# Three pairs of gate tiles as seven-product blocks, and two products of each block pair added up in PSUM

## The chip, the cores and the metric

One Trainium2 chip, one of its NeuronCores. The metric is the time of one execution on the device in microseconds (us), the median of some runs. A NeuronCore has TensorE (PE, the matrix array), VectorE (DVE), ScalarE (ACT), GpSimd (POOL) and SyncE (SP); each works through its own queue in order, and they wait for each other by semaphores. Matmuls read SBUF and add up in PSUM, which has 8 banks; DVE and ACT read PSUM, DMA queues move data between DRAM and SBUF.

## The reference

One encoder layer for 576 columns (512 frames of a prompt and 64 of a sample), model width 1024, FFN width 2816, all in fp32:

```python
x = x + 0.5 * swiglu_ffn(rms_norm(x, ffn1_norm), ffn1_w_gate_up, ffn1_w_down)
h = rms_norm(x, mix_norm)
p = h @ w_in
a_b, a_c, a_v, b_u, gate_a, gate_b = jnp.split(p, cuts, axis=-1)
a_conv, new_a = causal_depthwise_conv(a_c * a_v, hist_a, conv_a_w)
y_a = (a_b * a_conv) @ w_a_out
glu = b_u[..., :D_B] * jax.nn.sigmoid(b_u[..., D_B:])
b_conv, new_b = causal_depthwise_conv(glu, hist_b, conv_b_w)
b_act = jax.nn.silu(layer_norm(b_conv + conv_b_bias, conv_b_ln_g, conv_b_ln_b))
y_b = b_act @ w_b_out
merged = jax.nn.sigmoid(gate_a) * y_a + jax.nn.sigmoid(gate_b) * y_b
x = x + merged @ w_out
x = x + 0.5 * swiglu_ffn(rms_norm(x, ffn2_norm), ffn2_w_gate_up, ffn2_w_down)
```

and a last RMSNorm; the convolutions' last inputs are outputs too.

## The kernel before

Features lie on the 128 partitions, 8 tiles of 128 for the model width, the 576 columns along the free axis in two halves of 288. Weights are the stationary operand. For fp32 accuracy each operand is split into a high and a low part, and a product takes three matmuls: high x high, high x low, low x high. A **plain tile** (`product`: 128 output features, all 576 columns) is 8 x 3 x 2 = 48 matmuls of 288 columns, in one PSUM tile `mm` of two banks; the pool `mmps` has four of them. A finished product is put in the list `behind` and evacuated by `take` when the next one has been issued.

A **block pair** computes two output tiles by Winograd's form of Strassen's scheme: the weights of two tiles in 2 x 2 blocks (output tile by half of the 8 input tiles), the operand in 2 x 2 blocks (half of the input tiles by half of the columns), seven products (`block`, 12 matmuls into a single bank that `bank` hands out from two-bank tiles) in place of eight: 84 matmuls for 96. It needs sums of weight blocks (made on DVE for each pair as the weights come) and four sums of operand blocks, the forms, which the class `Forms` makes once for a stage: `combine` forms them on DVE and casts their high parts on ACT, `split` makes the low parts on DVE. Of the seven products q[0] to q[6] the two output tiles are put together from half tiles: the tile q1 is q[0] copied out by ACT, u2 comes of q[1] and q1, u4 of q[2] and u2, u3 of q[3] and u2; then a half of the first output comes of q[4] and q1 and its other half of q[5] and u4, a half of the second of q[2] and u3 and its other half of q[6] and u3, all on DVE. Semaphores guard PSUM by whole two-bank tiles.

The program runs in this order: FFN 1 (groups of gate/up tiles, of which 18 are block pairs, each followed by the down projection); branch b's value and gate tiles ("p", 4 and 3) and branch a's ("p", 1, 2, 0); then branch a's gate tiles ("p", 5, j) alternating with its output tiles ("ya", j); branch b's gate tiles ("p", 6, j); branch b's output "yb", two plain pairs and two block pairs; the output projection "o"; FFN 2 (21 block pairs). While PE works on the p and ya tiles, DVE runs branch b's 31-tap convolution and the LayerNorm behind it. These are small steps in the list `work`, which `fill` hands out between products by a planner's clock. The LayerNorm goes through `advance` in stages: gathering the sum, mean `mu`, then for each of 8 tiles `center` (subtract the mean on DVE, square on ACT, add to the running sum on DVE), the variance's sum on PE, and its reciprocal root; then `swish`.

The order on each engine is the order in which the code is written, kept by `Ordered`. Weights come through `Stream`: SP loads raw chunks to six buffers, ACT casts the high part, and the low part is made either by ACT (times -1) and an accumulating DMA that POOL issues, or by DVE; it works six units ahead of PE. All instructions go through one helper, so all have the line L88 in the profile; they are told apart by their tiles: `mm` PSUM, `tmp` work tiles, `u`, `g` and `act` homes of weights (`act` also of operands), `raw` loaded weights, `w` work tiles and sums of weights, `x` the residual and the merged outputs, `acc` running sums, `r` row factors.

Of the kernel before, what the change touches and what calls it, by code (L numbers as in the profile page):

```python
# [9 lines left out]
F32 = mybir.dt.float32  # L10
# [101 lines left out]
def tile_encoder_step(  # L112
# [280 lines left out]
    def plan_mixer(name, w, col, home_of=None, low="dma"):  # L393
        plan_tile(name, w, 0, (KU, KU), col, "act", home_of, low)
# [12 lines left out]
    for j in range(KT):  # L407
        plan_mixer(("p", 6, j), w_in, 6 * D + j * P, few)


# [38 lines left out]
            got += [(w, kk) for kk in range(ws.units[n][1])]  # L449
        return got  # L450

    def block(w, xs):

        q = bank()[:, :H]
        for k in range(KU):
            (whi, wlo), (xh, xl) = w, xs[k]
            for m, (l, r) in enumerate(((whi, xh), (whi, xl), (wlo, xh))):
                pe.matmul(q, l[:, k, :], r, start=k == m == 0, stop=k == KU - 1 and m == 2)
        return q


    work = []
# [180 lines left out]
    class Forms:  # L643
# [176 lines left out]
    def ffn(f, xg, sums, finish, forms, R=None, todo=()):  # L820
# [40 lines left out]
                    step(p)  # L861

        def pair(i, hs, last):
            qu, uu, t, cu = (ttile() for _ in range(4))
            q1, u2, u3, u4 = half(qu, 0), half(qu, 1), half(uu, 0), half(uu, 1)
            q = []

            def q7():
                dve.tensor_tensor(u3, q[3], u2, op=ALU.add)
                dve.tensor_tensor(half(cu, 1), u3, q[2], op=ALU.subtract)  # L870

            def gate():
                dve.tensor_tensor(half(t, 1), q[5], u4, op=ALU.add)
                dve.tensor_tensor(t, t, R, op=ALU.mult)
                sca.activation(t, t, AF.Silu)

            steps = (
                lambda: sca.copy(q1, q[0]),
                lambda: dve.tensor_tensor(u2, q[1], q1, op=ALU.subtract),
                lambda: dve.tensor_tensor(u4, q[2], u2, op=ALU.subtract),  # L880
                q7,
                lambda: dve.tensor_tensor(half(t, 0), q[4], q1, op=ALU.add),
                gate,
            )
            for n, xs in enumerate(bs):
                q.append(block(ws.get(plan[f, "s", i][n]), xs))
                if n > 0:
                    steps[n - 1]()
                if rest:
                    rest.pop(0)()  # L890

            hs.append(None)
            at = len(hs) - 1

            def up():
                if last:
                    dve.tensor_tensor(t, t, R, op=ALU.mult)
                dve.tensor_tensor(half(cu, 0), q[6], u3, op=ALU.add)
# [219 lines left out]
    def swish(i, RL, sig={}):  # L1118
# [13 lines left out]
        if 0 <= j < KT:  # L1132
            BA[j] = (BA[j], low(sig[j], BA[j]))
            forms.b.setdefault(j // 2, []).append(sig[j])

    def ga_of(j):
        def then(ps):
            t = gates[j] = ttile()
            sca.activation(halves(t), ps, AF.Sigmoid)
        return then  # L1140

    def ya_of(j):
        def then(ps):
            dve.tensor_tensor(halves(M[j]), ps, halves(gates.pop(j)), op=ALU.mult)
        return then

    stage, held = [0], [0]
# [1 line left out]
    def advance():  # L1149

        nonlocal var, mu, RL
        if stage[0] == 0 and len(C) == KT and not work:
            lnsum.gather()
        elif stage[0] == 1:
            mu = ttile()
            sca.mul(halves(mu), lnsum.total(), 1.0 / D)
            var = Sum()
            work.extend((lambda i=i: center(i, mu)) for i in range(KT))
        elif stage[0] == 2 and not work:
            var.gather()  # L1160
        elif stage[0] == 3 and not held[0]:
            held[0] = 1
            return
        elif stage[0] == 3:
            RL = rstd(var)
        else:
            return
        stage[0] += 1

    var = mu = RL = None  # L1170
    for j in range(KT):
        if j == 5:
            while len(C) < KT:
                work.pop(0)()
        product(("p", 5, j), xg, ga_of(j))
        advance()
        product(("ya", j), AB, ya_of(j))
        advance()
    take()
    sca.dma_start(hist.rearrange("(j p) n -> p j n", p=P), hst)  # L1180
    while stage[0] < 4:
        while work:
# [8 lines left out]
            work.append(lambda p=(i - 4) // 2: forms.split(p))  # L1191
    ws.ahead = 4

    def gb_of(j):
        def then(ps):
            while work and j >= 2 and len(BA) < j - 1:
                work.pop(0)()
            sg = wtile(n=T) if j < 2 else gtile(n=T)
            sca.activation(halves(sg), ps, AF.Sigmoid)
            SGB.append(sg)  # L1200
        return then

    for j in range(KT):
        product(("p", 6, j), xg, gb_of(j))
    while work:
        work.pop(0)()
# [32 lines left out]

    def block_pair(i):  # L1240
        j = 2 * i
        c1, c2, qu, uu = (ttile() for _ in range(4))
        q1, u2, u3, u4 = half(qu, 0), half(qu, 1), half(uu, 0), half(uu, 1)
        q = []

        def second():
            dve.tensor_tensor(u3, q[3], u2, op=ALU.add)
            dve.tensor_tensor(half(c2, 1), u3, q[2], op=ALU.subtract)

            if i == KU - 1:  # L1250
                MS[4], MS[5] = split(M[4]), split(M[5])

        def first():
            dve.tensor_tensor(half(c1, 1), q[5], u4, op=ALU.add)
            dve.tensor_tensor(c1, c1, SGB[j], op=ALU.mult)
            merged(j, c1)

        steps = (
            lambda: sca.copy(q1, q[0]),
            lambda: dve.tensor_tensor(u2, q[1], q1, op=ALU.subtract),  # L1260
            lambda: dve.tensor_tensor(u4, q[2], u2, op=ALU.subtract),
            second,
            lambda: dve.tensor_tensor(half(c1, 0), q[4], q1, op=ALU.add),
            first,
        )
        for n, xs in enumerate(bs):
            q.append(block(ws.get(plan["yb", "s", i][n]), xs))
            if n > 0:
                steps[n - 1]()
        dve.tensor_tensor(half(c2, 0), q[6], u3, op=ALU.add)  # L1270
        dve.tensor_tensor(c2, c2, SGB[j + 1], op=ALU.mult)
        merged(j + 1, c2)
        spare.clear()
# [164 lines left out]
```

## Time and profile before

| | |
|---|---|
| runs, median (lowest to highest) | 1294.61 us (1294.13 to 1297.48) |
| the profiled execution, its span | 1290.1 us |
| time beside the span, against the median | 4.5 us |
| mean granted TensorE clock | 0.997 |
| POOL busy | 361.6 us (28%) |
| DMA, mean | 167 GB/s |

The page gives each engine's busy time and share, then its busy tenths in 40 slices of the span; the views behind it group instructions by engine, operation and tile (count, busy time, mean ns of one, and the idle time before them with what ended it), list who waited for whom, follow the chain of work that ended last, show instructions in order of time (start, duration, what it is, and in brackets the idle time ahead of it and its releaser), and sum up busy times by stretches of time. Starts of matmuls are exact to follow PE's pace by; their ends overlap the next one's start.

### The profile page before, as it was taken

The numbers are of one execution on the slowest core, as the hardware profiler recorded it, in microseconds if no ns is written. First come the engines' busy times: TensorE is split into PE (matmuls) and PEld (weight loads), VectorE is DVE, ScalarE is ACT, GpSimd is POOL, SyncE is SP. The second block draws the span as 40 slices with busy tenths as digits, with TensorE's granted clock in tenths as the row PEclk, the third lists the DMA queues.
The fourth block names the chain that finished last, engine by engine and source line by source line (L and its number), as shares of the span: only waits on it lengthen the run. The fifth ranks groups of instructions, "written<-read, shape, count | busy, mean of one in ns | idle before, by whom it ended". The sixth has DMA issues, their size and how long they took to land.

```text
span 1290.1 us, 25702 instructions
## 1 busy us (share of the span) xinstructions
PE 1279.4 (99%) x9728; PEld 1277.5 (99%) x9728; DVE 925.1 (72%) x1539; ACT 765.5 (59%) x1359; POOL 361.6 (28%) x460
## 2 busy tenths in 40 slices
PE   9999999999999999999999999999999999999997
PEld 9999999999999999999999999999999999999997
DVE  6868668748846998888895166656867848847956
ACT  7655646646776645555444576477665655654664
POOL 0032332232333444333321221122142141241230
PEclk9999999999999999999999999999999999999998
DMA  7286787886799898788885767696687696796783
GB/s 220 70 181 154 163 180 155 177 181 149 154 224 232 174 200 173 165 172 174 172 172 124 163 142 154 151 236 145 139 175 171 151 197 151 164 204 138 158 172 97
DMA packets 286812, 215.26 MB, mean 167 GB/s; under 512 B 15456, under 2 KB 248928, under 8 KB 286688
## 3 DMA queue, kind: packets, MB, share of 16 engines
q0 software_dynamic: 56160, 92.43, 43.3%
q1 hardware_dynamic: 228784, 120.35, 32.8%
q8 instruction: 77, 1.26, 0.4%
q10 hardware_dynamic: 1744, 0.83, 0.2%
q14 instruction: 47, 0.39, 0.1%
HBM read 116.17 MB, written 4.98 MB: 94 GB/s over the span
## 4 chain that ended last, share of the span: by engine, by line
PE 92%; issue 4%; DVE 2%; DMA 1%; ACT 1%; POOL 0%; DVEq 0%; POOLq 0%; ACTq 0%
PE mm L88 92%; DVE tmp L88 0%; DMA g<-raw 0%; DMA raw<-in_w_b_out_dram 0%; DVE x L88 0%; DVE g L88 0%; DMA u<-raw 0%; ACT act L88 0%; DVE w L88 0%; POOL u L88 0%; DVE act L88 0%; ACT u L88 0%; ACT w L88 0%; ACT g L88 0%; POOL g L88 0%
## 5 line engine op out<-in xcount | busy, mean ns | idle before, releaser
L88 PE MATMUL mm<-act,u 128*128 128x288 f32 x4758 | 668.3, 293 | 0.1
L88 PEld LDWEIGHTS mm<-act,u 128*128 128x128 f32 x4758 | 638.9, 188 | 0.4 <-DMA u<-raw 0.3
L88 PE MATMUL mm<-act,g 128*128 128x288 f32 x3030 | 432.9, 294 | 0.9 <-DMA g<-raw 0.9
L88 PEld LDWEIGHTS mm<-act,g 128*128 128x128 f32 x3030 | 410.3, 188 | 1.1 <-DMA g<-raw 1.1
L88 POOL DMA_DIRECT2D u<-raw x197 | 172.3, 874 | 481.7 <-ACT u L88 317.4
L88 PE MATMUL mm<-act,act 128*128 128x288 f32 (+2 forms) x1896 | 259.9, 293 | 0.0
L88 PEld LDWEIGHTS mm<-act,act 128*128 128x128 f32 x1896 | 252.2, 188 | 0.5 <-ACT act L88 0.3
L88 ACT CAST u<-raw 128x512 fp32r<-128x512 f32 (+2 forms) x207 | 118.8, 574 | 172.0 <-PE mm L88 136.7
L88 POOL DMA_DIRECT2D g<-raw x126 | 109.9, 872 | 297.4 <-ACT g L88 242.7
L88 DVE SCALAR_TENSOR_TENSOR w<-g,prm,w 128x606 f32<-128x606 f32 x232 | 179.3, 844 | 1.4 <-ACT w L88 1.4
L88 DVE TENSOR_TENSOR tmp<-mm,tmp 128x288 f32<-128x288 f32 (+1 forms) x251 | 112.9, 459 | 70.3 <-PE mm L88 53.7
L88 ACT ACTIVATE u<-u 128x512 fp32r<-128x512 f32 (+2 forms) x197 | 116.8, 593 | 6.2
L88 ACT CAST g<-raw 128x512 fp32r<-128x512 f32 (+2 forms) x136 | 75.1, 553 | 43.9 <-DMA raw<-in_ffn_w_down_dram 17.6
L88 DVE SCALAR_TENSOR_TENSOR tmp<-mm,r 128x576 f32<-128x576 f32 x48 | 36.3, 757 | 76.6 <-PE mm L88 76.6
L88 POOL DMA_DIRECT2D act<-raw x67 | 59.1, 883 | 108.3 <-ACT act L88 94.5
L88 ACT CAST act<-tmp 128x576 fp32r<-128x576 f32 x92 | 61.9, 675 | 43.1 <-DVE tmp L88 42.1
L88 ACT CAST g<-w 128x512 fp32r<-128x512 f32 x79 | 49.0, 620 | 64.4 <-DVE w L88 58.6
L88 ACT CAST u<-w 128x512 fp32r<-128x512 f32 x81 | 50.2, 619 | 61.0 <-DVE w L88 43.6
L88 DVE TENSOR_TENSOR act<-tmp,act 128x576 fp32r<-128x576 f32 x92 | 67.5, 754 | 18.1 <-ACT act L88 16.5
L88 ACT ACTIVATE g<-g 128x512 fp32r<-128x512 f32 (+2 forms) x126 | 72.1, 572 | 4.0
L88 DVE TENSOR_TENSOR w<-raw,raw 128x512 f32<-128x512 f32 x82 | 56.2, 685 | 16.2 <-DMA raw<-in_ffn_w_gate_up_dram 11.2
L88 ACT ACTIVATE tmp<-tmp 128x576 f32<-128x576 f32 x47 | 32.2, 686 | 45.1 <-DVE tmp L88 45.0
(86 smaller groups left out, 830.6 us busy)
## 6 DMA issues: line engine op xcount, KB each, us to landing
raw<-in_ffn_w_gate_up_dram SPq DMA_DIRECT2D x171, 256.0 KB, 3.5
u<-raw POOLq DMA_DIRECT2D x140, 256.0 KB, 4.2
raw<-in_w_in_dram SPq DMA_DIRECT2D x112, 256.0 KB, 3.8
raw<-in_ffn_w_down_dram SPq DMA_DIRECT2D x96, 192.0 KB, 3.8
g<-raw POOLq DMA_DIRECT2D x69, 256.0 KB, 4.2
act<-raw POOLq DMA_DIRECT2D x61, 256.0 KB, 4.4
g<-raw POOLq DMA_DIRECT2D x43, 192.0 KB, 4.5
u<-raw POOLq DMA_DIRECT2D x41, 192.0 KB, 4.5
```

Of the source, the lines that this page charges most:

```text
L88: return self.tc.keep_in_program_order(fn(*args, **kwargs))
```

## The change

There are two parts. First, a new function `seven` runs the products of every block pair, and `block` can now be given a bank to add onto: product 4 is added to product 0's bank and product 5 to product 2's (the table `ONTO`). So that they can be, q[0] and q[2] are copied out first, by ACT. u4 is gone, and so is the addition for the first half of the first output: q[4]'s bank holds it, and ACT copies it out. A pair takes five banks in place of seven. DVE has two instructions less per pair, ACT two more. This holds for all pairs of FFN 1, yb and FFN 2.

Second, branch a's gate tiles ("p", 5, 2) to ("p", 5, 7) become three block pairs of the same kind. PE's order was p5 and ya in turn, then p6. It is now p5 tile 0, all eight ya, p5 tile 1, p6 tile 0, the three pairs, p6 tiles 1 to 7. The ya tiles from 1 on are copied out by ACT, and gated later on DVE (`gated`). The pairs' forms need the operand in one piece again: `whole` copies the high part with ACT and adds the low part by an accumulating DMA that POOL issues. The LayerNorm's stages behind the first now run between the products of the pairs (`between`).

```diff
@@ order of the weights @@
+    plan_mixer(("p", 5, 0), w_in, 5 * D)
     for j in range(KT):
-        plan_mixer(("p", 5, j), w_in, 5 * D + j * P)
         plan_mixer(("ya", j), w_a_out, j * P)
+    plan_mixer(("p", 5, 1), w_in, 5 * D + P)
+    plan_mixer(("p", 6, 0), w_in, 6 * D)
+    for i in range(1, KU):
+        plan_block(("p5", "s", i), [
+            ws.raw(w_in, h * KU * P, KU, 5 * D + j * P) for j in (2 * i + 1, 2 * i)
+            for h in range(2)
+        ], [home("act") for _ in range(7)])
@@ block and seven @@
-    def block(w, xs):
+    def block(w, xs, onto=None):
 
-        q = bank()[:, :H]
+        q = bank()[:, :H] if onto is None else onto
...
+    ONTO = {4: 0, 5: 2}
+
+    def seven(ws7, xs7, c1, c2, gate, between=None):
+        qu, uu = ttile(), ttile()
+        q1, u2, q3, u3 = half(qu, 0), half(qu, 1), half(uu, 0), half(uu, 1)
+        q = []
+
+        def second():
+            dve.tensor_tensor(u3, q[3], u2, op=ALU.add)
+            dve.tensor_tensor(half(c2, 1), u3, q3, op=ALU.subtract)
+
+        def first():
+            dve.tensor_tensor(half(c1, 1), q[5], u2, op=ALU.subtract)
+            gate()
+
+        steps = (
+            lambda: sca.copy(q1, q[0]),
+            lambda: dve.tensor_tensor(u2, q[1], q1, op=ALU.subtract),
+            lambda: sca.copy(q3, q[2]),
+            second,
+            lambda: sca.copy(half(c1, 0), q[4]),
+            first,
+        )
+        for n, xs in enumerate(xs7):
+            q.append(block(ws.get(ws7[n]), xs, q[ONTO[n]] if n in ONTO else None))
+            if n > 0:
+                steps[n - 1]()
+            if between:
+                between()
+        return lambda: dve.tensor_tensor(half(c2, 0), q[6], u3, op=ALU.add)
@@ Forms @@
+        def whole(self, p, xs):
+            self.b[p] = [wtile(n=T) for _ in range(2)]
+            for b, (hi, lo) in zip(self.b[p], (xs[p], xs[p + KU])):
+                sca.copy(b, hi.bitcast(F32))
+                pool.dma_start(b, lo.bitcast(F32), accum_op=ALU.add)
@@ the stage of p5, ya and p6 @@
-            mu = ttile()
+            mu = rpool.tile([P, T], F32, tag="r", name=nm("mu"), bufs=2)
...
+    xforms = Forms()
+    product(("p", 5, 0), xg, ga_of(0))
     for j in range(KT):
-        if j == 5:
+        if j == KT - 1:
             while len(C) < KT:
                 work.pop(0)()
-        product(("p", 5, j), xg, ga_of(j))
-        advance()
+            xforms.whole(0, xg)
         product(("ya", j), AB, ya_of(j))
-        advance()
-    take()
+        if stage[0] == 0:
+            advance()
+    for n, (b, then) in enumerate(((5, ga_of(1)), (6, gb_of(0)))):
+        for p in (2 * n, 2 * n + 1):
+            xforms.combine(p)
+            if p < KU - 1:
+                xforms.whole(p + 1, xg)
+            xforms.split(p)
+        product(("p", b, 1 - n), xg, then)
+    bs = xforms.operands(xg)
+    later = []
+
+    def gate_pair(i):
+        j = 2 * i
+        c1, c2 = ttile(), ttile()
+
+        def first():
+            sca.activation(c1, c1, AF.Sigmoid)
+            gated(j, c1)
+
+        def second():
+            final()
+            sca.activation(c2, c2, AF.Sigmoid)
+
+        def between():
+            take()
+            if later:
+                later.pop(0)()
+            advance()
+            fill()
+
+        final = seven(plan["p5", "s", i], bs, c1, c2, first, between)
+        later.extend((second, lambda: gated(j + 1, c2)))
```

What this does to the queues, at three places. On ACT of the changed kernel, behind tile ya5's evacuation: `x` rows are evacuations of ya tiles, the `COPY w<-act` rows are `whole`, and the `CAST act<-tmp` rows cast the forms that DVE makes from those `w`.

```order
L88 COPY x_96<-mm_8738 128x576
L88 CAST act_8874<-tmp_8868 128x576
L88 CAST act_8876<-tmp_8869 128x576
L88 COPY w_8878<-act_5268 128x576
L88 COPY w_8879<-act_5435 128x576
L88 CAST act_8894<-tmp_8888 128x576
L88 CAST act_8896<-tmp_8889 128x576
L88 COPY w_8898<-act_5271 128x576
L88 COPY w_8899<-act_5589 128x576
```

Nothing of this was there before; each round's copies stand behind the casts of the round ahead.

Further on in the same queue, from behind the last forms to the first gate pair's copy of q[0] (the last row): the `act` and `u` rows are weights, `tmp<-mm` and `w<-mm` the sigmoids of p5 tile 1 and p6 tile 0, `mu` the mean, `acc<-g` the first square.

```order
L88 CAST act_9007<-raw_8711 128x512
L88 ACTIVATE act_9008<-act_9007 128x512
L88 CAST u_9036<-w_9005 128x512
L88 ACTIVATE tmp_9062<-mm_8908 128x576
L88 CAST act_9072<-raw_8637 128x512
L88 ACTIVATE act_9073<-act_9072 128x512
L88 ACTIVATE w_9096<-mm_9003 128x576
L88 ACTIVATE mu_9098<-mm_9099 128x576
L88 ACTIVATE acc_9105<-g_5279 128x576
L88 CAST u_9110<-raw_8912 128x512
L88 ACTIVATE u_9110<-u_9110 128x512
L88 COPY tmp_9067<-mm_9083 128x288
```

Before, there were no pairs here, and the mean and the squares stood behind ya tiles; now eleven rows stand ahead of the copy. Between it and the copy of q[2] stand two more squares and two weight casts.

On DVE at the first yb pair, before (u2, then u4, then behind the sum `w<-raw,raw` of two weight blocks u3 and the half of the second output):

```order
L88 TENSOR_TENSOR tmp_10148<-mm_10162,tmp_10148 128x288
L88 TENSOR_TENSOR act_10194<-raw_10005,act_10193 128x512
L88 TENSOR_TENSOR tmp_10149<-mm_10196,tmp_10148 128x288
L88 TENSOR_TENSOR u_10213<-raw_10011,u_10213 128x512
L88 TENSOR_TENSOR w_10231<-raw_10158,raw_10160 128x512
L88 TENSOR_TENSOR tmp_10149<-mm_10196,tmp_10148 128x288
L88 TENSOR_TENSOR tmp_10147<-tmp_10149,mm_10196 128x288
```

and now (u2, the sum, u3, and the half of the second output from SBUF):

```order
L88 TENSOR_TENSOR tmp_10266<-mm_10280,tmp_10266 128x288
L88 TENSOR_TENSOR act_10312<-raw_10123,act_10311 128x512
L88 TENSOR_TENSOR u_10331<-raw_10129,u_10331 128x512
L88 TENSOR_TENSOR w_10349<-raw_10276,raw_10278 128x512
L88 TENSOR_TENSOR tmp_10267<-mm_10314,tmp_10266 128x288
L88 TENSOR_TENSOR tmp_10265<-tmp_10267 128x288
```

u4 is gone; u3 stands behind the same sum of weights as before.

More of the change, by code (lines that the diff above doesn't have):

```diff
@@ L1192, in tile_encoder_step @@
     ws.ahead = 4
[L1194 to L1203, printed above, removed]
+    for j in range(1, KT):
         product(("p", 6, j), xg, gb_of(j))
@@ L1241, in block_pair, with between @@
         j = 2 * i
[L1242 to L1251, printed above, removed]
+        c1, c2 = ttile(), ttile()
         def first():
[L1254 removed]
             dve.tensor_tensor(c1, c1, SGB[j], op=ALU.mult)
             merged(j, c1)
[L1258 to L1270, printed above, removed]
+        def between():
+            if i == KU - 1 and between.n == 4:
+                MS[4], MS[5] = split(M[4]), split(M[5])
+            between.n += 1
+        between.n = 0
+        seven(plan["yb", "s", i], bs, c1, c2, first, between)()
         dve.tensor_tensor(c2, c2, SGB[j + 1], op=ALU.mult)
```

57 lines of the change are left out of this document (33 added, 24 removed).

## The prediction, made before the changed kernel was run

> **What bounds the kernel now.** I read the page's head first, then PE's waits, then the chain of work that ended last.
>
> ```profile
> span 1290.1 us, 25702 instructions
> PE 1279.4 (99%) x9728; PEld 1277.5 (99%) x9728; DVE 925.1 (72%) x1539; ACT 765.5 (59%) x1359; POOL 361.6 (28%) x460
> PEclk9999999999999999999999999999999999999998
> PE mm L88 <- POOL eps L88: 1.0, 1, 1.0
> PE mm L88 <- DMA g<-raw: 0.9, 1, 0.9
> PE mm L88 <- ACT tmp L88: 0.5, 1, 0.5
> 4.81 803.97 PE mm L88 x6138
> ```
>
> PE is busy for 99% of the span, at full clock, and in all waits 2.4 us for anybody; the chain is PE without a break for its first 800 us. So time can be gained in two ways only, by fewer matmuls or faster ones, and **any new wait of PE is lost time, undiluted**. VectorE (DVE) and ScalarE (ACT) have slack on the mean, but the mean is not what counts where PE begins to wait for single instructions of theirs. The profiled execution's span is 1290.1 us; the median of the runs is 1294.61, so 4.5 us lie around the span, and I add them at the end.
>
> **Fewer matmuls.** A plain tile is 48 matmuls, a block pair 84 in place of 96. Their pace, in PE's timeline (start, duration, matmuls):
>
> ```profile
> 644.98 3.28 PE L88 MATMUL mm<-act,act 128*128 128x288 f32 x24
> 648.10 3.28 PE L88 MATMUL mm<-act,u 128*128 128x288 f32 x24
> 651.22 3.28 PE L88 MATMUL mm<-act,act 128*128 128x288 f32 x24
> ...
> 689.20 3.32 PE L88 MATMUL mm<-act,act 128*128 128x288 f32 x24
> 692.36 3.32 PE L88 MATMUL mm<-act,u 128*128 128x288 f32 x24
> 808.61 1.74 PE L88 MATMUL mm<-act,u 128*128 128x288 f32 x12
> ...
> 814.95 1.74 PE L88 MATMUL mm<-act,u 128*128 128x288 f32 x12
> 816.53 1.75 PE L88 MATMUL mm<-act,g 128*128 128x288 f32 x12
> ...
> 819.70 1.52 PE L88 MATMUL mm<-act,u 128*128 128x288 f32 x10
> ```
>
> Starts count, not the overlapping ends: a plain tile takes 651.22 - 644.98 = 6.24 us (130.0 ns a matmul), and 6.32 between the two four-matmul LayerNorm sums; a block pair takes 819.70 - 808.61 = 11.09 (132.0 ns). Two tiles become one pair: 11.09 - 12.48 = -1.39, three times. The four slow tiles between the sums were 0.08 slower each; that goes too. **-4.4 us**, and at 131.5 ns for each of the 36 matmuls it would be -4.7. That is sure, as far as PE is not made to wait.
>
> **What accumulating in PSUM moves.** DVE loses two instructions per pair, ACT gains two, in all 41 old pairs. Neither bounds. But before, block 4 wrote into a fresh bank, and now it is added onto the bank of product 0. It can't start until q1 has been copied out (ACT) and, where products 0 and 1 share a two-bank tile, until u2 has been computed (DVE); block 5 likewise waits for q3 and u3. Block 4 comes 6.34 us after the pair's start, block 5 7.92. So I ask where q1, u2 and u3 stood in each pair of before.
>
> First pair of FFN 1 (starts at 56.84), first yb pair (808.61) and first pair of FFN 2 (908.1; blocks 4 and 5 at 914.49 and 916.07):
>
> ```profile
> 63.17 1.74 PE L88 MATMUL mm<-act,g 128*128 128x288 f32 x12
> 63.41 0.39 ACT L88 COPY tmp<-mm 128x288 f32<-128x288 f32 x1
> 64.95 0.45 DVE L88 TENSOR_TENSOR tmp<-mm,tmp 128x288 f32<-128x288 f32 x1
> 818.56 0.69 DVE L88 TENSOR_TENSOR w<-raw,raw 128x512 f32<-128x512 f32 x1 [2.36 <-DMA raw<-in_w_b_out_dram]
> 819.17 0.45 DVE L88 TENSOR_TENSOR tmp<-mm,tmp 128x288 f32<-128x288 f32 x1
> 915.60 0.46 DVE L88 TENSOR_TENSOR tmp<-mm,tmp 128x288 f32<-128x288 f32 x1 [0.70 <-ACT tmp L88]
> 919.02 0.45 DVE L88 TENSOR_TENSOR tmp<-mm,tmp 128x288 f32<-128x288 f32 x1
> ```
>
> FFN 1: u2 ended at 65.40, block 4 began at 63.17: **+2.2**. yb: u3 (819.62) stands behind a sum of two weight chunks that came by DMA, block 5 began at 816.53: **+3.1**; the loads are not earlier in the changed order there. FFN 2: u2 ended at 916.06, 1.6 after block 4; u3, less the 0.37 of the subtraction that goes ahead of it, at 919.1, against a block 5 that is by then at 917.65: 1.4 more. **+3.0**. Each may be nothing, if its operand comes sooner than before, or half as long again.
>
> The other pairs, at the pair that starts at 1006.73 (blocks 4 and 5 at 1013.04 and 1014.62):
>
> ```profile
> 1011.58 0.46 DVE L88 TENSOR_TENSOR tmp<-mm,tmp 128x288 f32<-128x288 f32 x1 [0.56 <-ACT tmp L88]
> 1014.03 0.45 DVE L88 TENSOR_TENSOR tmp<-mm,tmp 128x288 f32<-128x288 f32 x1
> 1015.00 0.45 DVE L88 TENSOR_TENSOR tmp<-mm,tmp 128x288 f32<-128x288 f32 x1
> ```
>
> u2, u4, u3: u2 is 1.0 us ahead of block 4, but u3 ended at 1015.45, 0.83 late. u4 goes, which brings u3 0.37 forward; and the gate of the pair ahead, behind which u2 queues, no longer waits for a product in the other bank of its tile, some 1.3 us. I take **0** with 0.6 to spare; without that relief it is 0.46 in each of some 16 such pairs, +7 to +8.
>
> **The three gate pairs.** Here everything new meets: the operands' sums ("forms") are built late, the LayerNorm's steps are run between the products, and the evacuation of a pair sits behind both in ACT's and DVE's queues. Costs:
>
> ```profile
> u<-raw POOLq DMA_DIRECT2D x140, 256.0 KB, 4.2
> L88 ACT COPY tmp<-mm 128x576 f32<-128x576 f32 x8 | 5.0, 623 | 0.0
> L88 ACT CAST act<-tmp 128x576 fp32r<-128x576 f32 x92 | 61.9, 675 | 43.1 <-DVE tmp L88 42.1
> L88 DVE TENSOR_TENSOR tmp<-w,tmp 128x288 f32<-128x288 f32 x16 | 7.3, 454 | 0.3
> L88 ACT CAST act<-raw 128x512 fp32r<-128x512 f32 x65 | 39.7, 611 | 6.4 <-PE mm L88 3.0 <-DMA raw<-in_ffn_w_gate_up_dram 2.1 <-DMA raw<-in_w_in_dram 1.2
> L88 ACT ACTIVATE act<-act 128x512 fp32r<-128x512 f32 x61 | 38.6, 634 | 1.9
> 695.57 0.69 ACT L88 ACTIVATE tmp<-g 128x576 f32<-128x576 f32 x1 [1.49 <-DVE g L88]
> 696.29 0.76 DVE L88 TENSOR_TENSOR acc<-acc,tmp 128x576 f32<-128x576 f32 x1 [0.75 <-ACT tmp L88]
> 696.97 0.75 DVE L88 TENSOR_TENSOR g<-g,tmp 128x576 f32<-128x576 f32 x1
> ```
>
> *Forms.* Four rounds, each in series, since the next round's copies stand on ACT behind the casts of this one: two copies 1.25, the accumulating DMA's landing 4.2 (a transfer of weights of nearly this size; SBUF to SBUF as here), two DVE ops 0.91 until a cast can begin, two casts 1.35: 7.7 us. The first copy can't run before tile ya5 (ends at 644.98 + 7 x 6.24 = 688.7) is evacuated, a weight cast and a copy later, near 690.6. The last form is there at 690.6 + 4 x 7.7 = 721.4. PE reaches the pairs at 644.98 + 11 x 6.24 = 713.6, and block 1, the first to need the last form, at 715.2. That is a wait of about 6 us; with a landing of 3.3 it is 3.
>
> *Evacuation.* On ACT eleven instructions stand between the last form and the copy of q1: seven weight steps (0.61 and 0.63), two sigmoids, the mean and the first square (0.6 to 0.7 each), 6.9 us; the square waits about 1.5 more for its centering on DVE, which has weights ahead of it. Copy and u2 add 0.83: block 4 may go at about 730.6, where it stood ready at 726.9. u3 has five DVE ops (0.7 each) and a square behind it: 735.0. Pair 1 ends at 738.2, against 725 without a wait: 13.0. In the later pairs ACT has 18 ops (10.6 us) and DVE 20 (11.4 us) between one q1 and the next, as much as PE's 11.09, but they can't be packed: centering, square and running sum hand over from DVE to ACT and back (the rows above: 2.18 us a step, each engine idle for 0.75 or 1.49 of it). I followed both queues in their new order with these durations: pair 2 ends at 752.5 (3.2 late, u3 at its last block), pair 3 at 767.4 (3.8, u2, the variance's sum and u3), and the next gate tile waits 0.5 more for its bank. **+20.5 us**. From below: were the forms in time and each q1 the next thing on ACT, nothing; from above, all handed over in series, half as much again, 30.
>
> The outputs of branch a are now copied out by ACT and gated on DVE later, so 0.62 on ACT for each; between 680 and 700 it was busy for 9 us of 20:
>
> ```profile
> 680.00:700.00 20.00, 20.00 (x155) 20.00 (x155) 8.17 (x13) 9.03 (x16) 3.44 (x4) 1.00 0.59 126
> ```
>
> That hides them, **0**; their place in the queue is in the times above. The weights, loaded in the new order, I cost at nothing too: PE waited 0.9 us for them in all of before, and they run six units ahead; without that cover it would be a landing of 4.2.
>
> After the pairs, LayerNorm's output comes some 8 us later against the remaining gate tiles of branch b, whose evacuations it feeds: **+2**, 0 to 3.
>
> **The clock after a stall.** PE stands still twice in before: 1.16 us near 845, and at the very end (columns of the stretches: length, the five engines, clock, DMA):
>
> ```profile
> 845.00:845.50 0.50, 0.00 (x0) 0.00 (x0) 0.50 (x2) 0.47 (x2) 0.50 (x1) 1.00 1.05 194
> 1281.21 0.73 PE L88 MATMUL mm<-tmp,ones_r 128*128 128x272 f32 x2 [0.54 <-ACT tmp L88]
> 1283.00:1283.50 0.50, 0.00 (x0) 0.00 (x0) 0.47 (x2) 0.00 (x0) 0.00 (x0) 0.72 0.57 190
> 1283.50:1284.00 0.50, 0.00 (x0) 0.00 (x0) 0.47 (x2) 0.00 (x0) 0.00 (x0) 0.50 0.00 0
> ```
>
> Near 845 the clock stayed at 1.00; at the end it fell to half about 1.3 us after the last matmul (1281.94). The stalls above are longer than that. What the restart costs no row shows: nothing, or up to a whole block at half clock (another 1.58). Inside the gate pairs a slow block mostly runs into a later wait. For the three stalls outside I take as long at half clock as it took to fall, 0.65 each: **+2**.
>
> [...]
>
> **Sum**: -4.4 + 20.5 + 2 + 2.2 + 3.1 + 3.0 + 2 = +28.4. Span 1290.1 + 28.4 = 1318.5, time 1318.5 + 4.5 = **1323.0 us**.
>
> **The rivals.**
> *Faster: no operand is late.* It is decided at one place, block 4 of a gate pair: if q1's copy gets through ACT within 6.3 us of the pair's start, all pairs run at 11.09, and what remains is the 36 matmuls: 1290.2 us, 0.34% faster. For it: ACT is busy 59% and DVE 72%, and while PE waits once, the others catch up. Against: the order of ACT's queue, with eleven instructions ahead. **0.15**, spread over 1287 to 1297.
> *Partial.* The forms land in time (landing 3.3, weight casts ahead of them done early) and only the hand-overs remain, about 8 in the gate stage: -4.4 + 8 + 8 = 1306; 1297 to 1313. **0.20**.
> *Every second FFN pair waits* 0.46 for u3, because the relief by the bank fails: 7.5 more, 1330.5. u3's row above speaks for it, u4's removal against. **0.07**.
> *The clock gate.* Six restarts that nothing absorbs (three gate pairs, FFN 1, yb, FFN 2) run one block each at half clock, 6 x 1.58 = 9.5 in place of 2: 1330.5, and more if it takes longer. The row of the fall speaks for it, the one near 845 against it for short stalls. **0.11**.
> *The forecast*, 1313 to 1333: **0.47**.
>
> **How the numbers follow.** 0.3% is about what a measurement of this kernel can tell from no change, 1290.7 to 1298.5. Faster holds two thirds of the first rival: 0.10. Same holds the rest of it and the lower edge of the partial case: 0.07. Slower 0.83. The range goes from 1298 to 1340: it leaves out the first rival (0.15) and the upper tail of the clock's (0.03), and holds the bounds of the forms (17.5 to 23.5 in place of 20.5) and of FFN's steady pairs.
>
> **What would show it.** PE's waits in the new profile name the cause: ACT act or DVE act (forms) near 715, then ACT tmp and DVE tmp (q1, u2, u3) in 713 to 768, sum about 20; single waits for DVE tmp of 2 to 3 us at the first pairs of FFN 1, yb and FFN 2; and a granted clock below 1 behind them. PE's matmuls should be 36 fewer. The forecast is wrong if PE goes through the gate pairs without a gap (then 1290), or if PE's gaps lie in the FFN stages in every second pair.

## The result, and the profile after

The changed kernel takes 1332.12 us (median of 5 runs, 1328.62 to 1334.35) against 1294.13 us of before in the same session (5 runs, 1291.45 to 1297.48): a ratio of 1.029, 95% interval 1.027 to 1.031. Forecast were 1323.0, in a range of 1298 to 1340. It is slower by 38 us, where 28.4 were worked out.

The head of the page of the changed kernel, and PE's five longest waits in total (who was waited for, us in total, times, longest):

```profile
span 1327.7 us, 25642 instructions
PE 1286.0 (97%) x9692; PEld 1280.2 (96%) x9692; DVE 930.9 (70%) x1520; ACT 813.9 (61%) x1479; POOL 365.1 (27%) x465
PE mm L88 <- DVE tmp L88: 14.8, 10, 2.5
PE mm L88 <- ACT act L88: 8.8, 3, 6.7
PE mm L88 <- ACT tmp L88: 3.5, 3, 2.3
PE mm L88 <- DMA u<-raw: 3.5, 1, 3.5
PE mm L88 <- ACT u L88: 1.3, 1, 1.3
```

PE has 36 matmuls less, and 33.5 us of waits in all in place of 2.4. Nothing else of the head tells of it: DVE and ACT are as far from full as before. PE is "busy" for 6.6 us more with fewer matmuls; most of that is the clock, below.

Where the 37.6 us of the two profiled executions lie, by the starts of the same tiles in PE's timeline:

| from, to | before | after | difference | forecast |
|---|---|---|---|---|
| start to p5 tile 0 (FFN 1 in it) | 644.98 | 647.39 | +2.4 | +2.9 (2.2 + 0.65 of clock) |
| p5 tile 0 to p6 tile 1 (the gate pairs) | 107.47 | 130.19 | +22.7 | +16.1 (20.5 - 4.4) |
| p6 tile 1 to the first yb tile | 43.68 | 51.11 | +7.4 | +2 |
| yb to the output projection | 47.19 | 51.67 | +4.5 | +3.8 (3.1 + 0.65) |
| output projection to FFN 2's first pair | 64.83 | 63.08 | -1.7 | 0 |
| FFN 2's first pair to the end | 381.95 | 384.26 | +2.3 | +3.7 (3.0 + 0.65) |

The -1.7, which was not forecast, has two parts: before's wait near 845 (DMA g) is gone, 1.0 us, and most of the tiles go at 130.0 ns a matmul in place of 131.7 (see the end).

PE's timeline of the changed kernel through the first gate pair, blocks 0 to 6 and the LayerNorm's sum (start, duration, matmuls, in brackets the idle time ahead and its releaser):

```profile
716.03 1.74 PE L88 MATMUL mm<-act,act 128*128 128x288 f32 x12
717.61 0.69 PE L88 MATMUL mm<-tmp,ones_r 128*128 128x288 f32 x4
718.14 0.95 PE L88 MATMUL mm<-act,u 128*128 128x288 f32 x6
720.81 0.40 PE L88 MATMUL mm<-act,u 128*128 128x288 f32 x1 [1.72 <-ACT act L88]
721.60 0.53 PE L88 MATMUL mm<-act,u 128*128 128x288 f32 x2 [0.40 <-DVE act L88]
728.82 0.61 PE L88 MATMUL mm<-act,u 128*128 128x288 f32 x1 [6.70 <-ACT act L88]
...
732.80 3.25 PE L88 MATMUL mm<-act,act 128*128 128x288 f32 x12 [2.33 <-ACT tmp L88]
735.84 2.41 PE L88 MATMUL mm<-act,u 128*128 128x288 f32 x12
739.86 1.81 PE L88 MATMUL mm<-act,act 128*128 128x288 f32 x12 [1.60 <-DVE tmp L88]
744.11 3.25 PE L88 MATMUL mm<-act,u 128*128 128x288 f32 x12 [2.44 <-DVE tmp L88]
747.16 1.93 PE L88 MATMUL mm<-act,act 128*128 128x288 f32 x12
748.92 1.74 PE L88 MATMUL mm<-act,u 128*128 128x288 f32 x12
```

The waits come in the forecast's order: block 1 for the third and the fourth form (ACT act), block 4 for u2, block 5 for u3. One more, which the forecast did not name, lies between: block 2 waits for the bank that a sigmoid on ACT empties (ACT tmp). And blocks of the same 12 matmuls take 1.58 us from start to start, or up to 3.05 (744.11 to 747.16). The stretches of that time (length, PE, PEld, DVE, ACT, POOL, granted clock, DMA share, GB/s) say why:

```profile
733.00:737.00 4.00, 4.00 (x17) 4.00 (x18) 3.71 (x6) 3.14 (x6) 0.86 (x1) 0.50 0.47 100
750.00:757.00 7.00, 7.00 (x56) 7.00 (x55) 6.09 (x11) 4.57 (x9) 1.72 (x2) 1.00 0.62 121
```

Between 733 and 737 PE worked without a pause, but at half clock, 17 matmuls in 4 us where 30 go at full clock.

### The profile page after: what moved, and what is told of

The parts are those of the page before. It is cut to its first block, busy times and chain, and to the rows that moved or that the text cites. A ratio compares the mean times of both kernels' runs of the same rounds, so it can differ in the third digit from the quotient of the medians.

```text
span 1327.7 us, 25642 instructions
## 1 busy us (share of the span) xinstructions
PE 1286.0 (97%) x9692; PEld 1280.2 (96%) x9692; DVE 930.9 (70%) x1520; ACT 813.9 (61%) x1479; POOL 365.1 (27%) x465
## 4 chain that ended last, share of the span: by engine, by line
PE 85%; DVE 6%; issue 3%; ACT 3%; DMA 2%; POOL 0%; DVEq 0%; POOLq 0%; ACTq 0%
PE mm L88 85%; DVE tmp L88 2%; DMA w<-act 1%; DVE act L88 1%; ACT tmp L88 1%; DVE g L88 1%; ACT act L88 1%; DVE w L88 1%; DVE u L88 1%; ACT u L88 0%; ACT w L88 0%; DMA raw<-in_w_b_out_dram 0%; DVE x L88 0%; DVE acc L88 0%; DMA gains<-in_params_dram 0%
## 5 line engine op out<-in xcount | busy, mean ns | idle before, releaser
L88 POOL DMA_DIRECT2D g<-raw x123 | 107.2, 872 | 255.2 <-ACT g L88 153.1
L88 DVE TENSOR_TENSOR tmp<-mm,tmp 128x288 f32<-128x288 f32 (+1 forms) x181 | 83.9, 463 | 91.6 <-PE mm L88 63.0
L88 ACT CAST act<-tmp 128x576 fp32r<-128x576 f32 x100 | 67.4, 675 | 68.6 <-DVE tmp L88 67.0
L88 DVE TENSOR_TENSOR act<-tmp,act 128x576 fp32r<-128x576 f32 x100 | 73.5, 754 | 16.0 <-ACT act L88 14.4
L88 ACT CAST u<-w 128x512 fp32r<-128x512 f32 x86 | 53.2, 619 | 49.4 <-DVE w L88 34.8
L88 ACT COPY tmp<-mm 128x288 f32<-128x288 f32 (+1 forms) x140 | 56.5, 404 | 41.4 <-PE mm L88 37.4
L88 DVE TENSOR_TENSOR w<-raw,raw 128x512 f32<-128x512 f32 x88 | 60.3, 685 | 25.8 <-DMA raw<-in_ffn_w_gate_up_dram 13.0
```

The costliest lines, as they stand in the source:

```text
L88: return self.tc.keep_in_program_order(fn(*args, **kwargs))
```

## The experiments

Twelve kernels were run, in five sessions; each ratio is against runs of the kernel before on the same chip, with its 95% interval.

### The two parts apart

`acc_old` is the kernel before with `seven` and `ONTO` in its 41 block pairs and nothing else. `seven_banks` is the changed kernel with

```diff
-    ONTO = {4: 0, 5: 2}
+    ONTO = {}
...
-            lambda: sca.copy(q3, q[2]),
+            lambda: dve.tensor_tensor(u4, q[2], u2, op=ALU.subtract),
             second,
-            lambda: sca.copy(half(c1, 0), q[4]),
+            lambda: dve.tensor_tensor(half(c1, 0), q[4], q1, op=ALU.add),
```

> The kernel before with the first part of the change alone: products 4 and 5 added up in PSUM in the 41 old block pairs, no gate pairs. Theory A (a bank that is added onto is given back late, and PE waits where DVE or ACT is behind): the three places of the changed kernel come back alone, waits of PE for DVE tmp of 1.9 us in FFN 1, 2.6 in yb and 1.7 and 1.4 in FFN 2, and some 2 us at a lower clock behind them, less about 1 because the gap near 845 falls away: 1301 to 1304 us, 0.6% over before. Rival B (adding up costs nothing, all of the loss comes from the gate pairs and the new order): within 0.2% of before, and no waits of PE for DVE tmp.

> The changed kernel with the second part of the change alone: gate pairs, forms and order as changed, but all 44 pairs with seven banks each and the old steps on DVE. A: the waits at the first pairs of FFN 1, yb and FFN 2 go (9 us with the clock), and in the gate pairs the waits for DVE tmp go (about 9 us), while those for the forms (ACT act and DVE act, 10 us) and for the weights behind the pairs (5 us) stay: 1312 to 1318. B: the waits come from the queues, not from the banks; they stay where they were: 1328 to 1334.

| | median us | ratio to before |
|---|---|---|
| acc_old | 1302.98 | 1.0083 (1.0058 to 1.0109) |
| seven_banks | 1319.09 | 1.0213 (1.0185 to 1.0242) |

The two ratios are worth 10.7 and 27.5 us; together 38.2, and the whole change 37.5. By the spans of the profiled executions it is 8.5 and 25.5, together 34.0, and the whole change 37.6. So the parts add up within some 5 us, which is what the intervals leave open; that neither feeds the other at all is not shown. PE's waits, first of acc_old, then of seven_banks:

```profile
PE mm L88 <- DVE tmp L88: 7.8, 5, 2.5
```

```profile
PE mm L88 <- ACT act L88: 7.8, 2, 6.7
PE mm L88 <- ACT tmp L88: 6.6, 3, 3.7
PE mm L88 <- DMA u<-raw: 4.3, 2, 2.8
PE mm L88 <- DMA act<-raw: 2.7, 1, 2.7
```

In acc_old the waits for DVE tmp are at the first pairs of FFN 1, yb and FFN 2 and one in yb's second pair (0.4); none in the other pairs. Rival B falls: adding up in PSUM costs, though only where DVE or ACT is behind. With seven banks DVE tmp is all but gone from the gate stage too (0.3 in all), but the waits for ACT tmp rose from 3.5 to 6.6 us, a bank that an ACT evacuation holds and the LayerNorm's sum, and weights of the second pair are late. So A was right on the three places outside, while of its 9 us in the gate pairs nothing came back: from p5 tile 0 to p6 tile 1 it takes 129.9 us in place of 130.2, other operands being late instead. The time is 1 us over A's range.

### The forms

`forms_early` starts the rounds two tiles earlier, with two rounds' copies in flight; `both` does that with seven banks. `whole_dve` leaves the rounds where they were and makes them without a DMA:

```diff
-                sca.copy(b, hi.bitcast(F32))
-                pool.dma_start(b, lo.bitcast(F32), accum_op=ALU.add)
+                dve.tensor_tensor(b, hi.bitcast(F32), lo.bitcast(F32), op=ALU.add)
```

> The changed kernel with the forms' rounds begun two tiles earlier, one round ahead of each of the tiles ya6, ya7, p5 1 and p6 0, with two rounds' copies in flight. A: PE's waits for ACT act and DVE act (10 us) go; the evacuation of the pairs still queues behind the LayerNorm's steps, so waits for DVE tmp stay, and the three places outside stay: 1316 to 1324. Rival C (the forms alone are what is late in the gate stage, the rest follows from them): all 27 us of that stage go, 1303 to 1307.

> Early forms and seven banks together. A: only the weights behind the pairs are left (7 us with the clock), and part of the LayerNorm's hand-overs: 1293 to 1302. If the gate pairs' matmuls were slower in themselves (rival D: accumulation or not, a block costs more here than 131 ns a matmul), it would be over 1305.

> The changed kernel with the operand put together by one DVE addition (0.75 us) in place of ACT's copy and POOL's accumulating DMA; nothing else moved. Theory A (the landing is what made a round 9.1 us in place of 7.7): a round falls to about 4 us, PE's waits for ACT act (8.8 us) go, and the evacuation queue behind them moves up by as much, as in forms_early: 1313 to 1322. Rival F (a round's length is set by ACT's casts and their place in the queue): rounds stay over 7 us and the time over 1327.

| | median us | ratio to before |
|---|---|---|
| forms_early | 1316.36 | 1.0183 (1.0150 to 1.0216) |
| both | 1303.62 | 1.0095 (1.0064 to 1.0127) |
| whole_dve | 1313.22 | 1.0152 (1.0125 to 1.0179) |

In forms_early no wait for ACT act is left, and the time is within A's range, against C: with the forms in time, the evacuation is late all the same, 13.2 us of waits for DVE tmp in the whole kernel. The gate pairs' stage falls from 130.2 to 115.1 us. `both` came out 1.6 us over its range: PE waited 4.1 us for ACT tmp and 6.9 for weights (DMA u and DMA act), all in the gate stage and behind it, and 33 matmuls went at half clock there, 3.6 us more. Its gate pairs' stage takes 115.0 us: with the forms in time, too, seven banks gain nothing there, but 4.4 us in the p6 tiles behind it and 11.5 in the other stages. whole_dve shows what made the rounds long. On ACT of the changed kernel they stand out (`CAST act<-tmp` the casts of a round, `COPY w<-act` the next round's copies):

```profile
700.55 1.41 ACT L88 CAST act<-tmp 128x576 fp32r<-128x576 f32 x2 [1.87 <-DVE tmp L88]
701.87 1.24 ACT L88 COPY w<-act 128x576 f32<-128x576 f32 x2
709.68 1.41 ACT L88 CAST act<-tmp 128x576 fp32r<-128x576 f32 x2 [6.57 <-DVE tmp L88]
711.00 1.24 ACT L88 COPY w<-act 128x576 f32<-128x576 f32 x2
...
720.08 1.41 ACT L88 CAST act<-tmp 128x576 fp32r<-128x576 f32 x2 [5.75 <-DVE tmp L88]
721.40 1.24 ACT L88 COPY w<-act 128x576 f32<-128x576 f32 x2
728.10 1.41 ACT L88 CAST act<-tmp 128x576 fp32r<-128x576 f32 x2 [5.46 <-DVE tmp L88]
```

From cast to cast it is 9.1, 10.4 and 8.0 us. And in whole_dve, where one DVE addition stands for copy and DMA, they are 3.1, 6.0 and 4.3 apart, though a weight cast that waits for PE stands in between:

```profile
699.08 1.25 ACT L88 CAST act<-tmp 128x576 fp32r<-128x576 f32 x2
702.17 1.42 ACT L88 CAST act<-tmp 128x576 fp32r<-128x576 f32 x2 [1.84 <-DVE tmp L88]
...
708.20 1.41 ACT L88 CAST act<-tmp 128x576 fp32r<-128x576 f32 x2 [0.26 <-DVE tmp L88]
712.47 1.41 ACT L88 CAST act<-tmp 128x576 fp32r<-128x576 f32 x2 [2.86 <-DVE tmp L88]
```

The last forms are cast by 713.9 in place of 729.5, and the time is in A's range, though 1.4 us of waits for ACT act are left. F falls. The edit takes out ACT's copies, 1.2 us a round, together with the DMA; the rows above tell them apart, since most of a round lies between the end of the copies and the casts.

### The clock

`filler` is acc_old with 12 matmuls more: block 3 of the first yb pair is computed twice, into the same bank.

```diff
             q.append(block(w, xs, q[ONTO[n]] if n in ONTO else None))
+            if n == 3 and ws7 is plan["yb", "s", 1]:
+                block(w, xs, q[3], again=True)
```

> acc_old with block 3 of the first yb pair computed twice, 12 matmuls (1.58 us) more, ahead of the wait there. Theory A (PE's stall of 2.6 us brings the clock down, and the 16 matmuls behind it then take 240 ns in place of 131): the wait shrinks to about 1 us, the clock stays at 1.00, and the kernel is 1.7 us shorter for more work: 1300.5 to 1302. Rival G (the clock falls for another reason, or after shorter stalls too): as acc_old within 0.3 us, with 240 ns a matmul behind the wait.

It takes 1300.77 us, in A's range, ratio 1.0054 (1.0034 to 1.0073), against acc_old's 1.0083. The intervals overlap and the two ran on different chips, so the verdict is the trace's: from the first yb tile to the output projection filler takes 50.52 us and acc_old 52.27, 1.75 less for 1.58 us more of work. PE's timeline from block 5 on, first acc_old, then filler:

```profile
821.42 2.75 PE L88 MATMUL mm<-act,g 128*128 128x288 f32 x12 [2.48 <-DVE tmp L88]
823.98 2.42 PE L88 MATMUL mm<-act,act 128*128 128x288 f32 x12
826.24 3.34 PE L88 MATMUL mm<-act,u 128*128 128x288 f32 x24
```

```profile
822.05 1.85 PE L88 MATMUL mm<-act,g 128*128 128x288 f32 x12 [0.86 <-DVE tmp L88]
823.73 1.74 PE L88 MATMUL mm<-act,act 128*128 128x288 f32 x12
825.31 3.28 PE L88 MATMUL mm<-act,u 128*128 128x288 f32 x24
```

Behind the wait of 2.48 us two blocks take 826.24 - 821.42 = 4.82 us, behind one of 0.86 us 3.26. In acc_old 15 matmuls there take 240 ns and the clock reads 0.50 between 823 and 825; in filler it stays at 1.00 there. So A holds in yb: the stall brought the clock down, and cost 1.6 us on top of itself. But G's second half, that shorter stalls do it too, holds elsewhere in the same run, in filler's FFN 1:

```profile
64.45 2.35 PE L88 MATMUL mm<-act,g 128*128 128x288 f32 x12 [2.12 <-DVE tmp L88]
66.60 2.83 PE L88 MATMUL mm<-act,u 128*128 128x288 f32 x12
69.27 1.74 PE L88 MATMUL mm<-act,g 128*128 128x288 f32 x12
```

Two blocks take 69.27 - 64.45 = 4.82 us again, and the clock reads 0.50 between 65.6 and 68.9. In acc_old the same blocks, behind a wait of the same 2.12 us, start at 64.98, 66.66 and 68.24, 3.26 us for two, and the clock stays at 1.00. whole_dve and clock_set show the drop in FFN 1 too (2.12 and 2.09 us); behind FFN 2's waits (1.6 and 1.2) the clock stays at 1.00 in acc_old and in the changed kernel.

So the length alone doesn't decide. In these traces the clock changes in steps of 3.41 us: a stretch at half clock lasts 3.41 us (822.05 to 825.47 in acc_old, 65.57 to 68.99 in filler, 744.14 to 747.55 in the changed kernel) or a whole multiple (723.66 to 737.31, four, in the changed kernel), and the changed kernel's nine changes, from 723.66 to 1320.99, all lie on one grid of that step. Filler's wait in FFN 1 lies within one step (62.16 to 65.57); in acc_old it is split over two, 1.44 and 0.69 us. In the changed kernel the clock fell behind the five steps at full clock in which PE was idle for 1.92, 1.99, 2.44, 2.49 and 3.25 us, and behind none with 1.60 or less; at the end of before it fell behind one with 1.8. By these traces, then, the same stall costs 1.6 us more or nothing, by where it falls on the grid.

A stretch of 3.41 us at half clock, with PE busy all through it, loses an estimated 1.7 us by its length; 1.6 were measured. The grid lies differently in each execution: its first edge behind the span's start is at 3.2 us in before, 0.0 in the changed kernel, 2.9 in acc_old and 0.7 in filler, counted back from the changes at 1283.22, 723.66, 822.05 and 65.57 in steps of 3.4133 us (856.78 to 1320.99 in the changed kernel is 136 of them).

### The order of the LayerNorm, and the planner

`ln_first` lets the LayerNorm's stages run from the last ya tiles on (`advance()` behind every plain tile), with early forms and seven banks; `ln_first_acc` does the same with products added up in PSUM. `clock_set` is the changed kernel with one line, behind the gate pairs:

```diff
+    dve.time = max(dve.time, pe.time)
     for i in range(KT + 2):
         work.append(lambda i=i: swish(i, RL))
```

> Early forms, seven banks, and the LayerNorm's stages run between the last ya tiles, p5 1 and p6 0 as far as they are ready, in place of between the gate pairs' products. A: with nothing but weights and evacuations left in ACT's and DVE's queues the gate pairs run without a wait, and the p6 tiles behind them too; the 4.7 us of matmuls come through: 1286 to 1292, at or below before. Rival E (the weights of three pairs in a row can't be made in time, whatever else stands in the queues): waits for DMA u and DMA act of 4 to 7 us stay: 1294 to 1300.

> The same with products 4 and 5 added up in PSUM. A: q1 is then the next thing on ACT, so the gate pairs still wait for nothing, and only the three places of the other stages come back, 9 to 11 us over ln_first. B: a bank that is added onto costs in the gate pairs as well, waits for DVE tmp between 715 and 750, 15 us or more over ln_first.

> The changed kernel with one line more: behind the gate pairs the planner's time of DVE is set to PE's, as every plain product's evacuation does it and the pairs do not. Theory A (the waits of 5.1 us for weights in the p6 tiles, ACT u and DMA u, come from a dozen swish steps handed out at once, since the planner thinks DVE idle): they go, with the 2 us of low clock behind them, 1324 to 1328, and the rest stays. Rival H (the LayerNorm's end is too late there, wherever the steps stand): waits of 4 us or more stay between 780 and 830, or move to the first yb tile.

| | median us | ratio to before |
|---|---|---|
| ln_first | 1313.53 | 1.0161 (1.0137 to 1.0186) |
| ln_first_acc | 1328.54 | 1.0269 (1.0243 to 1.0295) |
| clock_set | 1326.66 | 1.0255 (1.0229 to 1.0282) |

ln_first came out 21 us over A's range and 13 over E's. E's waits for weights were there (DMA u 4.2, DMA act 1.6), and its pairs had 4 us of waits in all; but two others were new: 4.8 us for the variance's sum, which PE reached before ACT and DVE had its terms, and 8.0 us (ACT u) in the p6 tiles. ACT at that time, columns as above:

```profile
785.92 1.41 ACT L88 CAST act<-tmp 128x576 fp32r<-128x576 f32 x2 [0.86 <-DVE tmp L88]
787.23 0.61 ACT L88 CAST u<-raw 128x512 fp32r<-128x512 f32 x1
```

From 769 on there are steps of `work` alone (swish and yb's forms), most of them waiting for DVE, and the weight cast for which PE stands comes at 787. `fill` hands out a step while the planner's time of DVE is behind PE's; a pair moves PE's time on and not DVE's, so that after three pairs the planner took DVE for idle and gave out nearly all steps at once. In the changed kernel it is the same: the waits for ACT u and DMA u, 4.8 us, are of these tiles. clock_set takes away the one for ACT u, and 2.8 us of 3.5 for DMA u stay. From p6 tile 1 to the first yb tile it takes 47.4 us in place of 51.1, half of the 7.4 lost there. 1.2 of these 3.7 us are half-clock matmuls (2 in place of 13), and by the clock's steps they went by chance: the wait of 2.77 us is split over two of them, 1.36 and 1.41. The medians don't settle it, since its interval and the changed kernel's overlap (1.0229 to 1.0282, 1.027 to 1.031). So A is right on the lump for a part; what stays is less than H's 4 us, and I didn't take it apart.

ln_first_acc is 15 us over ln_first by the medians, 12.5 by the spans. The three places outside make 8.0 of the 12.5 (FFN 1 2.3, yb 2.7, FFN 2 3.0; the clock stays at 1.00 behind yb here). The gate pairs' stage is 2.4 longer, with two waits of over half a microsecond for DVE tmp (2.0 and 0.6), and the p6 tiles 2.2. So B holds in part: a bank that is added onto can cost there too, 2.4 us in this comparison, against 0.3 and 0.1 in the two above (seven_banks, and `both` against forms_early), where other operands were late.

### Three versions after what was found

`tuned` puts together seven banks, whole_dve's addition, a round of forms ahead of each of ya6, ya7, p5 1 and p6 0, the LayerNorm first with its running sum one step behind the squares and the variance's sum held back for six products, and clock_set's line. `tuned2` makes the pairs' low weight parts on DVE and works six units ahead in p6; `tuned3` has the forms one tile earlier, and weights eight units ahead in the pairs.

> The gate pairs with everything that the runs so far point to: seven banks; the operand put together by DVE; one round of forms ahead of each of ya6, ya7, p5 1 and p6 0; LayerNorm ahead of the pairs, its running sum one step behind the squares, and its variance's sum on PE six products later; the planner's time set behind the pairs. A: nearly all waits are gone, 1287 to 1294, so that at last the 36 matmuls show. Rival E (three pairs' weights in a row are late by themselves): 4 us or more of waits for DMA u and DMA act between 730 and 760, 1294 to 1300.

> tuned with the low parts of the gate pairs' weights made by DVE in place of ACT's product and POOL's DMA, and six units ahead in the p6 tiles as elsewhere in place of four. A: the 5.5 us of waits for weights left in tuned (DMA act 3.0, DMA u 1.4 and small ones) go: 1286 to 1291, a ratio of 0.994 to 0.998. Rival E: DVE is late with them now, and PE waits for DVE act or DVE u in place of the DMAs: 1292 to 1297, ratio 1.00.

> tuned with each round of forms one tile earlier, and weights made eight units ahead in the gate pairs and six in the p6 tiles (low parts by ACT and POOL's DMA, as in tuned). A: the waits left in tuned (5.5 us, all for weights and the last form) go: 1286 to 1291, a ratio of 0.994 to 0.998. Rival E: with more units ahead ACT is only busier earlier, the waits move ahead of the pairs, and the ratio stays within 0.998 to 1.002.

| | median us (12 runs) | before (17 runs) | ratio to before |
|---|---|---|---|
| tuned | 1293.65 | 1294.47 | 0.9999 (0.9986 to 1.0013) |
| tuned2 | 1293.41 | 1291.16 | 1.0007 (0.9994 to 1.0020) |
| tuned3 | 1291.52 | 1291.39 | 0.9993 (0.9980 to 1.0006) |

The 38 us are gone, but none is faster than before by what can be measured. tuned's time is in A's range; the ratios that A gave for tuned2 and tuned3 were missed, and both ratios lie where E put them. PE's waits sum to 5.9 us in tuned, 5.6 in tuned2 (DVE act 1.7 of it, as E had said), and in tuned3 PE's whole list is:

```profile
PE mm L88 <- POOL eps L88: 1.0, 1, 1.0
PE mm L88 <- ACT w L88: 0.9, 1, 0.9
PE mm L88 <- DVE u L88: 0.8, 1, 0.8
PE mm L88 <- DMA act<-raw: 0.6, 2, 0.4
PE mm L88 <- ACT tmp L88: 0.5, 1, 0.5
PE mm L88 <- DVE tmp L88: 0.2, 1, 0.2
PE mm L88 <- DMA u<-raw: 0.2, 1, 0.2
```

These are 4.2 us, 1.8 more than before, so that of the 4.7 us of matmuls some 2.9 should be left, 0.2%. That lies within the intervals, and its profiled execution (span 1292.4, 2.3 over before's 1290.1) went the other way, by PE's pace: up to p5 tile 0 it is 2.7 us longer with hardly a wait more, see the end.

## Why the prediction was right, point by point

**What bounds** held: PE's waits and its clock make up all of the loss, while DVE's and ACT's shares hardly moved.

**Fewer matmuls, -4.4** (4.5 by its own terms). Blocks that wait for nothing go at 131.5 ns as worked out (748.92 to 750.50 in the gate pairs, 1.58 us for 12). The gain can't be seen by itself in the changed kernel; the tuned versions, which have the same matmuls, show no gain clear of the noise.

**The banks' three places.** By PE's starts (the profile's idle times are some 0.2 shorter) FFN 1 lost 1.9 us (2.2 forecast), for DVE tmp; yb 2.6 (3.1); FFN 2 1.7 and 1.4 (1.6 and 1.4). acc_old shows them alone. The other FFN pairs don't wait, as taken; the rival with 0.46 us in each falls.

**The gate pairs, 20.5.** The mechanism held, the size was 27.2 (130.19 us, less 11 plain tiles of 6.24, two sums of 0.53 and three pairs of 11.09). By PE's starts 22.7 of it are waits, and some 4 are matmuls at half clock, which the forecast had put at next to nothing here, since a slow block would run into a later wait. That the waits came within 2.2 us is in part luck. Pair 1 waited 17.1 us in place of 13.0: block 1 10.0 for the forms (about 6 forecast), then block 2 2.6 for its bank (no place of the forecast's), block 4 1.8 for u2 (3.7) and block 5 2.6 for u3. Pair 2 waited 1.6 in place of 3.2, pair 3 and the tile behind it 4.0 in place of 4.3.

The term that was mis-sized is the round of the forms: 9.2 us on the mean in place of 7.7. The first copy ran at 692.98, which less the 2.4 us lost before is the forecast's 690.6; the last form was there at 728.8 in place of 721.4 + 2.4. The median landing of these DMAs was 4.1 us, as the 4.2 taken. But a round has two of them, and the casts wait for the second: from the end of the copies to the casts it took 6.6 (703.11 to 709.68), 7.8 and 5.5 us in the rows above, where 4.2 and 0.9 had been taken. POOL issued the second 0.9 us behind the first in the last two of these rounds and 2.8 in the one before, and the DVE operations that read them started 1.8 to 3.6 us apart; why the second lands so late was not tested.

**After the pairs, +2**, was 7.4: the bound of 3 was too low. The cause that was named (the LayerNorm's output comes late) is not the one that clock_set shows for a part of it: the planner gave out the steps in one lump, and ACT's weight casts stood behind them.

**The clock, +2.** A restart cost 1.6 us (yb in acc_old, FFN 1 in filler), not 0.65, but of the three stalls outside only yb's brought the clock down; that FFN 1's did not is luck: in clock_set, which is the same kernel up to there, it did. In the gate pairs half-clock matmuls took some 4 us more, in the p6 tiles 1.4. In all it is 7 us in place of 2.

**What I added for the time around the span, 4.5 us,** was wrong in kind: in each run whose span is listed 1.7 to 2.1 us lie around it (1329.53 and 1327.7). The rest of the 4.5 is how far the runs of before spread, 1289.67 to 1296.25 in the last sessions.

**The rivals.** The faster one falls by its own condition: block 4 of the first gate pair waited. Even in tuned3, where hardly an operand is late, the time is that of before and not 0.34% under it, though with 1.8 us more of waits only 0.2% was left to show. The partial case, forms in time and the hand-overs left, is forms_early and whole_dve: 1316 and 1313, above its range and at the end of it. The FFN pairs' rival falls, since no other pair waits. The clock's had the nearer sum, 9.5 against the 7 measured, but there were four restarts, not six.

## What to carry to other kernels

Where one engine is busy all the time, a change that saves it a few instructions is worth those and no more, while each new wait costs its whole length (here 31.1 us of new waits in 37.6 of loss), and one of some 2 us may bring a slow restart on top (1.6 us behind 2.48 in acc_old's yb, 1.6 behind 2.12 in filler's FFN 1): count the waits first. Adding up in a PSUM bank that must be emptied first ties PE to the newest result of the evacuating engines in place of one some blocks old (7.8 us of waits for DVE tmp in acc_old); look for the places where these are behind, at the starts of stages. And a planner that hands out work by a clock of its own has to move that clock on for every new kind of step.

## What the runs showed of the hardware that had not been expected

**PE's pace has two values** for the same plain tiles, 130.0 and 131.7 ns a matmul, and keeps one for long stretches. The same shapes in the same stage, just ahead of 650 us, in the profiled execution of tuned (before's, in the prediction, start 3.12 apart):

```profile
644.17 3.32 PE L88 MATMUL mm<-act,u 128*128 128x288 f32 x24
647.33 3.32 PE L88 MATMUL mm<-act,act 128*128 128x288 f32 x24
```

Here they start 3.16 apart, at a granted clock of 1.00 in both. In this part of before the slow pace lay between the two LayerNorm sums (there are more such stretches, from 850 to 900 for one); in tuned it held up to the first of them, at 691.58, and gave way to 130.0 there. It lasted from 401 on, where before's tiles go at 130.0; over 290 us that is 3.7 us, nearly as much as the 36 matmuls. What sets it at the start of a stretch stays open; I made no run for it. It may be the spread of before's runs, too; that is not shown.

**A stall's price** is in the section on the clock: the same 2.12 us of waiting made 1.6 us of slow matmuls behind it in one execution and none in another, by its place among the steps of 3.41 us in which the clock changes.
